# Second mixer of a four-part encoder: exchanging channel rows and step rows by block DMAs instead of TensorE transposes

## The chip, the cores and the metric

The kernel runs on one core of a Trainium2 chip. The metric is the device time of one execution in microseconds (us). Before the change three runs gave a median of 1613.68 us (1609.65 to 1622.86).

Engines are named as the profile names them: PE is TensorE's matmul, PEld its weight load, DVE is VectorE, ACT is ScalarE, POOL is GpSimd. SP issues every DMA of this stage, in one order.

## The reference, cut to what matters

Two layers, each a mixer, cross-attention and a ConvFFN, on 512 steps of 1024 channels. The change lies in the mixer of the second layer:

```python
def mixer_cd(hn, ...):
    u_c, h_d = split_sizes(hn @ w_in, (C_WIDTH, 2 * D_WIDTH))      # 512 and 1024 channels
    u = u_c.reshape(Bn, S, C_NGROUPS, C_GROUP)                     # 32 groups of 16 channels
    y_f = s5_scan(u, ...)                                          # s_t = a s_(t-1) + B u_t ; y_t = Re(C s_t)
    y_b = flip(s5_scan(flip(u), ...))                              # the same backwards
    y = (y_f + y_b).reshape(Bn, S, C_WIDTH) + d_skip * u_c
    z = gelu(y)
    o_c = z * sigmoid(z @ w_glu + b_glu)
    val, gate = split(h_d, 2)                                      # conformer part
    u = depthwise_conv(val * sigmoid(gate), conv_w, conv_b)        # 31 taps
    o_d = silu(layernorm(u, ln_g, ln_b))
    return concatenate([o_c, o_d]) @ w_out
```

All arithmetic is in float32; the large products split each operand into a high and a low part and use three matmuls.

## The kernel before, in words

Activations lie with channels in the 128 partitions and the 512 steps along the free axis. The 512 channels of each part are four blocks of 128 (index i, 0 to 3). In `mixer_cd` a table `CD` (lines 82 to 87) is read from left to right; each entry is a letter (a step) and a digit (the block), and the first instruction that a step puts on PE and on SP is tied behind the last one traced there, so the table sets the order on these two engines. A scheduler orders the rest; the DVE taps (`q`) are tied on DVE.

The letters that matter here, for block i:

- `u`: projection (24 matmuls of 512 columns) of S5's input, scaled on DVE into `uT` (line 1327). `v`, `V` and `g`, `G`: the same for the value and the gate of the conformer part; the gated product ends on DVE at line 1447.
- `a` and `b`: the scan works on pieces of 8 steps. For it a row must be one of 8 steps times 16 channels of a group, and a column one of 64 pieces, eight groups side by side. `a` makes eight transposes on PE (`chunks`, line 1336) with two evictions by ACT (line 1337), `b` eight more (`steps_`, line 1345) with one eviction into `Rg` (line 1353).
- `c`, `C`: 16 matmuls (line 1374) on `Rg`, eviction to `T`, two DMAs that swap the halves of `T` (lines 1378 and 1379), then eight DVE instructions with the scan (lines 1380 to 1388). `s` swaps halves again by DMA (`X2s`, lines 1394 and 1395), `x` adds (line 1402, on POOL for three of the eight).
- `y`: 24 matmuls (lines 1416 and 1418) give S5's output, evicted by ACT. `f` transposes it back, eight transposes (`channels`, line 1425), adds the skip on DVE (line 1431) and applies gelu on ACT (line 1433).
- `q`: two taps of the depthwise convolution of blocks 0 and 1 on DVE, in the channel layout (line 1463). Blocks 2 and 3 go through PE instead: `A` and `B` transpose as `a` and `b` do, `Z` (twice a block) makes 20 matmuls (line 1489) with a table `ct`, `F` transposes back (line 1425) and adds the bias on ACT (line 1497). `N` sums the four blocks for the layernorm's mean (lines 1505 to 1509).
- `l`, `L`, `m`, `w` load tables by DMA (`bm`, `cst`, `cm`, `ct`). `k` is one step of the next cross-attention's keys and values: eight of 12 matmuls of 512 columns (weights `in_w_xv`), then eight of 24 matmuls of 256 columns (`in_w_xk`). These depend on nothing in the mixer.

Weights of 512 KB arrive through three buffers `wr` (line 147). Their DMAs stand in a fixed order among SP's other DMAs. ACT rounds a weight to the high part `wh` (line 201), DVE or POOL makes the low part `wl` (line 202), and PE then uses it (lines 206 to 208). SP issues in order: while a DMA waits for its data, all that stand behind it wait too.

Of the kernel before, what the change touches and what calls it, by code (L numbers as in the profile page):

```python
# [12 lines left out]
F32R = mybir.dt.float32r  # L13
# [6 lines left out]
S = 512  # L20
# [70 lines left out]
def trunk(ctx, tc, xT, memT, pos, vec, amask, cmask, bmask,  # L91
# [9 lines left out]
    n_ = [0]  # L101
# [1156 lines left out]
    def mixer_cd(norm, nnext, kv):  # L1258
# [6 lines left out]
        def k4(shape, tag, bufs, dt=F32):  # L1265
            return T.tile(shape, dt, tag=tag, bufs=bufs, name=nm(tag))
# [3 lines left out]
        g3 = lambda v: v.rearrange("p (g c) -> p g c", c=64)  # L1270
        xp = [T.tile([128, 8, 65], F32, name=f"xp{j}") for j in range(2)]
# [57 lines left out]
        def chunks(src):  # L1329

            us = src.rearrange("p (c t) -> p t c", t=8)
            at = k4([64, 8, 8, 16], "at", 3)
            for hf in range(2):
                tp = tp_ps()
                for t in range(4):
                    PE.transpose(tp[:64, 128 * t:128 * t + 128], us[:, 4 * hf + t], ident)
                A.activation(at[:, :, 4 * hf:4 * hf + 4].rearrange("c g t k -> c t g k"),
                             tp[:64].rearrange("c (t g k) -> c t g k", t=4, k=16), AF.Copy)
            return at

        def steps_(at):

            rp = sc_ps()
            for g in range(8):
                PE.transpose(rp[:, 64 * g:64 * g + 64], at[:, g].rearrange("c t k -> c (t k)"), ident[:64, :64])
            return rp
# [63 lines left out]
        def y_(i):  # L1410
            At[i] = k4([64, 8, 8, 16], "at", 3)
            for hf in range(2):
                yp = sc_ps()
                for g in range(4):
                    o, gg = yp[:64, 128 * g:128 * g + 128], 4 * hf + g
                    PE.matmul(o, Rg[i][:, 64 * gg:64 * gg + 64], cm[i][0][:, gg], start=True, stop=False)
                    for d in range(2):
                        PE.matmul(o, X[i, d][:, gg, d:d + 64], cm[i][1 + d][:, gg], start=False, stop=d == 1)
                A.activation(At[i][:, :, 4 * hf:4 * hf + 4].rearrange("c t g k -> c g t k"),
                             yp[:64].rearrange("c (g t k) -> c g t k", g=4, k=16), AF.Copy)  # L1420

        def channels(at):
            yq = sc_ps()
            for t in range(8):
                PE.transpose(yq[:, 64 * t:64 * t + 64], at[:, t].rearrange("c g k -> c (g k)"), ident[:64, :64])
            return yq
# [110 lines left out]
        stage = {"u": (PS_, u_), "a": (PS_, a_), "b": (PS_, b_), "x": ((), x_), "y": (PS_, y_),  # L1537
# [4 lines left out]
                 "A": (PS_, ca_), "B": (PS_, cb_), "w": (PS_, w_), "Z": (PS_, z_), "q": ((V,), q_), "F": (PS_, cf_), "N": (PS_, n_),  # L1542
# [8 lines left out]
        for i in range(4):  # L1551
            split(hg[i], uT[i])
        for i in range(4):
# [8 lines left out]
            V.scalar_tensor_tensor(sgm, sgm, 1.0, uT[i], op0=ALU.add, op1=ALU.mult)  # L1562
            o_t[i] = k4([128, 2, S], "at" if i < 2 else "bm", 3 if i < 2 else 2, F32R)
# [78 lines left out]
def _col(v):  # L1642
    return np.asarray(v, np.float32).reshape(-1, 128).T


def layout(inp):
# [87 lines left out]
```

## Time and profile before

| | |
|---|---|
| median of three runs | 1613.68 us |
| the profiled execution, its own time | 1613.46 us |
| its span (first to last instruction) | 1611.7 us |
| PE busy | 1562.1 us, 97% |
| PEld busy | 1307.9 us, 81% |
| DVE busy | 1077.3 us, 67% |
| ACT busy | 708.3 us, 44% |
| POOL busy | 358.7 us, 22% |
| granted TensorE clock over the span | 0.984 |
| DMA | 189.11 MB, 117 GB/s on average |

Busy shares are averages over stages with different limits; a matmul's busy time overlaps its neighbours'. What one costs in a stream is the distance from its start to the next one's. `mixer_cd`'s work on PE runs from about 866 us to 1110 us of the span, the part that the change touches from about 874 us to 1062 us.

### The profile page before, as it was taken

The numbers are of one execution on the slowest core, as the hardware profiler recorded it, in microseconds if no ns is written. First come the engines' busy times: TensorE is split into PE (matmuls) and PEld (weight loads), VectorE is DVE, ScalarE is ACT, GpSimd is POOL, SyncE is SP. The second block draws the span as 40 slices with busy tenths as digits, with TensorE's granted clock in tenths as the row PEclk, the third lists the DMA queues.
The fourth block names the chain that finished last, engine by engine and source line by source line (L and its number), as shares of the span: only waits on it lengthen the run. The fifth ranks groups of instructions, "written<-read, shape, count | busy, mean of one in ns | idle before, by whom it ended". The sixth has DMA issues, their size and how long they took to land. (4 is left out here: it accounts for less than half of the span.)

```text
span 1611.7 us, 20961 instructions
## 1 busy us (share of the span) xinstructions
PE 1562.1 (97%) x8036; PEld 1307.9 (81%) x8036; DVE 1077.3 (67%) x1479; ACT 708.3 (44%) x1089; POOL 358.7 (22%) x367
## 2 busy tenths in 40 slices
PE   8999999999999999999999988989999999999997
PEld 6787889888888787777788877978888888888887
DVE  7576766466568789579746997375745766636644
ACT  5464755354444443234336342374534444414423
POOL 8411000000059853553510111110000101100101
PEclk9999999999999999999999998999999999999998
DMA  5322333231223335435454685452302322232331
GB/s 178 109 72 86 118 105 118 66 121 63 66 80 100 111 111 152 144 116 164 126 166 172 218 276 172 150 177 91 106 27 79 105 97 100 92 105 92 89 109 64
DMA packets 76117, 189.11 MB, mean 117 GB/s; under 512 B 8368, under 2 KB 27440, under 8 KB 76016
## 3 DMA queue, kind: packets, MB, share of 16 engines
q1 hardware_dynamic: 75376, 186.58, 36.1%
q8 instruction: 63, 1.03, 0.3%
q0 software_dynamic: 320, 1.05, 0.2%
q14 instruction: 38, 0.31, 0.1%
q10 hardware_dynamic: 320, 0.13, 0.0%
HBM read 162.43 MB, written 19.01 MB: 113 GB/s over the span
## 5 line engine op out<-in xcount | busy, mean ns | idle before, releaser
L201 ACT ACTIVATE wh<-wr 128x1024 fp32r<-128x1024 f32 (+1 forms) x229 | 239.2, 1045 | 430.3 <-PE mm L207 324.2
L208 PE MATMUL mm<-hg,wl 128*128 128x512 f32 x1000 | 394.9, 395 | 12.3 <-DVE wl L202 10.9
L206 PE MATMUL mm<-hg,wh 128*128 128x512 f32 x1000 | 399.2, 399 | 4.6 <-ACT wh L201 4.6
L207 PE MATMUL mm<-hg,wh 128*128 128x512 f32 x1000 | 393.6, 394 | 0.0
L202 DVE TENSOR_TENSOR wl<-wr,wh 128x1024 fp32r<-128x1024 f32 (+1 forms) x219 | 285.7, 1305 | 73.7 <-ACT wh L201 71.6
L208 PEld LDWEIGHTS mm<-hg,wl 128*128 128x128 f32 x1000 | 190.3, 190 | 56.6 <-DVE wl L202 13.7
L206 PEld LDWEIGHTS mm<-hg,wh 128*128 128x128 f32 x1000 | 190.7, 191 | 46.5 <-ACT wh L201 5.0
L207 PEld LDWEIGHTS mm<-hg,wh 128*128 128x128 f32 x1000 | 190.4, 190 | 40.4 <-issue 1.4
L208 PE MATMUL mm<-g,wl 128*128 128x512 f32 x324 | 126.7, 391 | 3.2 <-DVE wl L202 3.1
L206 PE MATMUL mm<-g,wh 128*128 128x512 f32 x324 | 126.9, 392 | 0.0
L207 PE MATMUL mm<-g,wh 128*128 128x512 f32 x324 | 126.2, 389 | 0.0
L976 POOL TENSOR_TENSOR t<-t,t 128x512 f32<-128x512 f32 x22 | 28.9, 1315 | 427.6 <-ACT t L182 427.6
L968 DVE TENSOR_TENSOR u<-mm,R 128x512 f32<-128x512 f32 x88 | 60.3, 688 | 73.8 <-PE mm L208 73.6
L970 ACT ACTIVATE t<-u,vt 128x512 f32<-128x512 f32 x88 | 70.8, 807 | 42.9 <-DVE u L968 42.6
L986 DVE TENSOR_TENSOR h<-mm,h 128x512 f32<-128x512 f32 x40 | 27.6, 691 | 87.7 <-PE mm L208 87.7
L971 DVE SCALAR_TENSOR_TENSOR t<-u,vt,t 128x511 f32<-128x511 f32 x88 | 77.8, 885 | 7.9 <-ACT t L970 7.9
L972 DVE SCALAR_TENSOR_TENSOR t<-u,vt,t 128x511 f32<-128x511 f32 x88 | 76.8, 872 | 4.0 <-DMA dct<-tr 1.4
L208 PEld LDWEIGHTS mm<-g,wl 128*128 128x128 f32 x324 | 60.8, 188 | 16.8 <-DVE wl L202 4.0
L182 ACT ACTIVATE t<-t 128x512 f32<-128x512 f32 x44 | 27.8, 632 | 102.3 <-DVE t L972 102.2
L207 PEld LDWEIGHTS mm<-g,wh 128*128 128x128 f32 x324 | 60.8, 188 | 12.5
L206 PEld LDWEIGHTS mm<-g,wh 128*128 128x128 f32 x324 | 60.9, 188 | 12.4
L202 POOL TENSOR_TENSOR wl<-wr,wh 128x1024 fp32r<-128x1024 f32 x10 | 25.3, 2531 | 148.4 <-ACT wh L201 148.4
(522 smaller groups left out, 3020.2 us busy)
## 6 DMA issues: line engine op xcount, KB each, us to landing
wr<-in_w_up SPq DMA_DIRECT2D x88, 512.0 KB
wr<-in_w_dn SPq DMA_DIRECT2D x32, 448.0 KB
wr<-in_w_ab SPq DMA_DIRECT2D x16, 512.0 KB
wr<-in_w_xv SPq DMA_DIRECT2D x16, 512.0 KB
wr<-in_w_xk SPq DMA_DIRECT2D x16, 512.0 KB
wr<-in_w_xq SPq DMA_DIRECT2D x16, 512.0 KB
wr<-in_w_xo SPq DMA_DIRECT2D x16, 512.0 KB
wr<-in_w_dn SPq DMA_DIRECT2D x16, 512.0 KB
```

Of the source, the lines that this page charges most:

```text
L182: tabbed(A.activation(dst, src, fn, **kw))
L201: A.activation(H[:, :n], raw[:, :n], AF.Copy)
L202: (eng or V).tensor_tensor(L[:, :n], raw[:, :n], H[:, :n].bitcast(F32), ALU.subtract)
L206: PE.matmul(ps, lH, rH, start=start, stop=False)
L207: PE.matmul(ps, lH, rL, start=False, stop=False)
L208: PE.matmul(ps, lL, rH, start=False, stop=stop)
L968: V.tensor_tensor(u, ps, R, ALU.mult)
L970: A.activation(t, u, AF.Identity, scale=vc(f"cw{l}", 44 + i), bias=vc(f"cb{l}", i))
L971: V.scalar_tensor_tensor(t[:, 1:], u[:, :S - 1], vc(f"cw{l}", i), t[:, 1:], op0=ALU.mult, op1=ALU.add)
L972: V.scalar_tensor_tensor(t[:, :S - 1], u[:, 1:], vc(f"cw{l}", 88 + i), t[:, :S - 1], op0=ALU.mult, op1=ALU.add)
L976: (V if l == 0 else G).tensor_tensor(res[1], res[1], res[0], ALU.mult)
L986: V.tensor_tensor(h[c], ps, h[c], ALU.add)
```

## The change

Channels are put into another order within each block (row 8k+g instead of 16g+k for group g, channel k), by reordering the weights and vectors on the host. The steps of `uT` are stored with the place in the piece outermost. A block copy of 16 rows by 8 groups by 64 columns then exchanges rows of channel and rows of step, so `forth` and `back` are eight DMAs each, issued by SP. The transposes and their evictions go. `y` and `Z` take the tables as the stationary operand and the data as the moving one (64 columns instead of 128), and write 128 rows. `e` and `E` are new letters (the way back); `b` and `B` go. DVE and ACT take over the reordering of steps where they read or write. `CD` is written anew.

```diff
 CD = """
-l0 L0 K0 u0 v0 V0 g0 a0 G0 b0 k1 u1 c0 C0 m0 q0 k1 a1 v1 V1 l1 q0 q0 s0 L1 b1 k1 g1 G1 x0 q0 q0 c1 C1 k1 q0 u2 q0 y0
-l2 q0 q1 a2 q1 k1 s1 q0 f0 L2 q1 v2 m1 q0 V2 x1 b2 q1 q0 g2 q0 G2 q1 c2 C2 A2 k1 q0 q1 y1 q0 k1 m2 B2 w2 q1 u3 s2 L3 q0 q1
...
+l0 L0 K0 u0 v0 V0 a0 g0 G0 k1 u1 c0 C0 m0 q0 k1 a1 v1 V1 l1 q0 q0 s0 L1 k1 g1 G1 x0 q0 q0 c1 C1 k1 q0 u2 q0 y0
+l2 q0 q1 k1 a2 q1 s1 q0 L2 q1 v2 m1 q0 V2 x1 e0 q1 q0 g2 q0 G2 q1 f0 c2 C2 k1 A2 q0 q1 y1 q0 k1 m2 w2 q1 u3 s2 L3 q0 q1
...
         def u_(i):
...
-            V.tensor_tensor(uT[i], ps, R, ALU.mult)
...
+            V.tensor_tensor(ct3(uT[i]), tc3(ps), tc3(R), ALU.mult)
+        def forth(dst, src):
+            for t in range(8):
+                nc.sync.dma_start(dst[16 * t:16 * t + 16], src[:, 64 * t:64 * t + 64])
+
+        def back(dst, src):
+            for t in range(8):
+                nc.sync.dma_start(dst[:, 64 * t:64 * t + 64], g3(src[16 * t:16 * t + 16]))
 
         def a_(i):
-            At[i] = chunks(uT[i])
-
-        def b_(i):
             Rg[i] = b2("Rg", 4)
-            A.activation(Rg[i], steps_(At[i]), AF.Copy)
+            forth(g3(Rg[i]), uT[i])
...
         def y_(i):
...
+            yp = sc_ps()
+            for g in range(8):
+                o = yp[:, 64 * g:64 * g + 64]
+                PE.matmul(o, cm[i][0][:, g], Rg[i][:, 64 * g:64 * g + 64], start=True, stop=False)
+                for d in range(2):
+                    PE.matmul(o, cm[i][1 + d][:, g], X[i, d][:, g, d:d + 64], start=False, stop=d == 1)
+            At[i] = b2("sh", 3)
+            A.activation(At[i], yp, AF.Copy)
+
+        def e_(i):
+            y = b2("sd", 2)
+            back(y, At[i])
+            At[i] = y
 
         def f_(i):
-            us = uT[i].rearrange("p (c t) -> p t c", t=8)
-            yq = channels(At[i])
-            V.scalar_tensor_tensor(us, us, vc("s5_d", i), yq.rearrange("p (t c) -> p t c", t=8),
-                                   op0=ALU.mult, op1=ALU.add)
-            A.activation(uT[i], uT[i], AF.Gelu_apprx_tanh)
+            V.scalar_tensor_tensor(uT[i], uT[i], vc("s5_d", i), At[i], op0=ALU.mult, op1=ALU.add)
+            A.activation(Rg[i].rearrange("p (c t) -> p c t", t=8), uT[i].rearrange("p (t c) -> p c t", t=8),
+                         AF.Gelu_apprx_tanh)
...
-            V.scalar_tensor_tensor(dv[i], g, 1.0, dv[i], op0=ALU.add, op1=ALU.mult)
+            if i < 2:
+                V.scalar_tensor_tensor(dv[i], g, 1.0, dv[i], op0=ALU.add, op1=ALU.mult)
+            else:
+                Bt[i] = b2("sh", 3)
+                V.scalar_tensor_tensor(ct3(Bt[i]), tc3(g), 1.0, tc3(dv[i]), op0=ALU.add, op1=ALU.mult)
...
         def ca_(i):
-            Bt[i] = chunks(dv[i])
-
-        def cb_(i):
-            A.activation(vg[i % 2][:, :, 2:66], g3(steps_(Bt[i])), AF.Copy)
+            forth(vg[i % 2][:, :, 2:66], Bt[i])
...
+        def ce_(i):
+            y = b2("sd", 2)
+            back(y, Bt[i])
+            Bt[i] = y
 
         def cf_(i):
-            yq = channels(Bt[i])
             accs[i] = b2("dv", 6)
-            A.activation(accs[i].rearrange("p (c t) -> p t c", t=8), yq.rearrange("p (t c) -> p t c", t=8),
+            A.activation(accs[i].rearrange("p (c t) -> p c t", t=8), Bt[i].rearrange("p (t c) -> p c t", t=8),
                          AF.Identity, bias=vc("conv_b", i))
...
+    q = np.arange(512).reshape(4, 8, 16).transpose(0, 2, 1).reshape(512)
```

SP's order around the weight of `v3` (the first `in_w_cd` below), before the change; `X2s` is the second swap of block 2, `cst` and `bm` are tables of block 3:

```order
L147 DMA wr_8159<-in_w_xv 128x1024
L1394 DMA X2s_8192<-T1s_8015 64x512
L1395 DMA X2s_8192<-T1s_8015 64x512
L1394 DMA X2s_8195<-T1s_8038 64x512
L1395 DMA X2s_8195<-T1s_8038 64x512
L1363 DMA cst_8198<-dct_0_118 128x1024
L1363 DMA cst_8200<-dct_1_119 128x1024
L147 DMA wr_8217<-in_w_cd 128x1024
```

The same place in the changed kernel; `sd` is the way back of `y1`, `Rg` the way forth of `u3`:

```order
L147 DMA wr_8096<-in_w_xv 128x1024
L1339 DMA sd_8199<-sh_8057 128x1x64 x7
L1335 DMA Rg_8165<-uT_8127 16x8x64 x3
L1384 DMA X2s_8129<-T1s_7969 64x512
L1385 DMA X2s_8129<-T1s_7969 64x512
L1335 DMA Rg_8165<-uT_8127 16x8x64
L1384 DMA X2s_8132<-T1s_7992 64x512
L1385 DMA X2s_8132<-T1s_7992 64x512
L1353 DMA cst_8135<-dct_0_118 128x1024
L1353 DMA cst_8137<-dct_1_119 128x1024
L147 DMA wr_8143<-in_w_cd 128x1024
```

Eleven block DMAs, four of which wait for `uT` of block 3, now stand ahead of that weight.

SP's order around the last `in_w_xv` weight, before the change:

```order
L1394 DMA X2s_8518<-T1s_8359 64x512
L1395 DMA X2s_8518<-T1s_8359 64x512
L1394 DMA X2s_8521<-T1s_8382 64x512
L1395 DMA X2s_8521<-T1s_8382 64x512
L147 DMA wr_8548<-in_w_xv 128x1024
```

The same place in the changed kernel; `vg` is the way forth of the gated product of block 3 (`sh`, written at line 1436, which answers to line 1447 before):

```order
L1385 DMA X2s_8423<-T1s_8281 64x512
L1335 DMA vg_7313<-sh_8385 16x8x64 x8
L1384 DMA X2s_8423<-T1s_8281 64x512
L1384 DMA X2s_8426<-T1s_8304 64x512
L1385 DMA X2s_8426<-T1s_8304 64x512
L147 DMA wr_8453<-in_w_xv 128x1024
```

The last weight of this kind, and three of the four swaps of block 3, now stand behind DMAs that wait for the gate's product.

PE's order around the mean's matmul (on `T` and `ones`), before the change; `hg` are matmuls of the GLU:

```order
L206 MATMUL mm_8888<-hg_89,wh_8865 128x512
L207 MATMUL mm_8888<-hg_89,wh_8865 128x512
L208 MATMUL mm_8888<-hg_89,wl_8866 128x512
L1509 MATMUL sc_8834<-T_1456_8830,ones 128x512
L206 MATMUL mm_8913<-hg_86,wh_8909 128x512
```

In the changed kernel; `mg` are matmuls of the last key step ahead of it:

```order
L207 MATMUL mm_8738<-mg_7735,wh_8734 128x256
L208 MATMUL mm_8738<-mg_7735,wl_8735 128x256
L1498 MATMUL sc_8770<-T_1434_8766,ones 128x512
L206 MATMUL mm_8805<-hg_86,wh_8801 128x512
L207 MATMUL mm_8805<-hg_86,wh_8801 128x512
```

Before, 24 matmuls of the GLU stand ahead of the mean's; now none does, and a key step stands in their place.

## Rows read from the trace of the kernel before

**Rows 1.** The page, part 1: busy time, share of the span, instructions.

```profile
PE 1562.1 (97%) x8036; PEld 1307.9 (81%) x8036; DVE 1077.3 (67%) x1479; ACT 708.3 (44%) x1089; POOL 358.7 (22%) x367
```

**Rows 2.** Windows: length, busy PE, PEld, DVE, ACT, POOL, granted clock, DMA share, GB/s.

```profile
890.00:976.00 86.00, 78.94 (x451) 64.70 (x450) 84.36 (x118) 32.81 (x50) 11.20 (x5) 0.96 0.72 245
957.00:976.00 19.00, 12.84 (x53) 9.21 (x52) 18.17 (x24) 6.42 (x9) 4.89 (x2) 0.82 0.65 222
```

**Rows 3.** Waits of PE, 860 to 1110 us: total, times, longest.

```profile
PE mm L206 <- ACT wh L201: 3.5, 1, 3.5
PE tp L1336 <- DVE dv L1447: 2.8, 1, 2.8
```

**Rows 4.** Timeline of PE: start, duration, line, out<-in, shapes, count.

```profile
875.02 1.03 PE L1336 MATMUL tp<-ident,uT 128*64 128x128 f32 x8
875.81 0.48 PE L206 MATMUL mm<-hg,wh 128*128 128x512 f32 x1
...
878.73 0.71 PE L1345 MATMUL sc<-ident,at 64*128 64x64 f32 x8
879.36 0.50 PE L206 MATMUL mm<-hg,wh 128*128 128x512 f32 x1
...
884.94 3.68 PE L1374 MATMUL tp<-Rg,bm 128*128 128x64 f32 x32
...
1025.52 4.53 PE L1489 MATMUL sc<-ct,vg 128*64 128x128 f32 x40
```

**Rows 5.** Timeline of SP: block copies of 64 KB in a row; a pair of swaps.

```profile
828.89 4.37 SPq L1210 DMA_DIRECT2D dmt<-kl  x7
...
986.43 0.59 SPq L1379 DMA_DIRECT2D T1s<-T  x1
```

**Rows 6.** Timeline of DVE: the instruction that waited for that pair.

```profile
989.51 0.69 DVE L1380 TENSOR_TENSOR T<-T,cst 128x512 f32<-128x512 f32 x1 [0.40 <-DMA T1s<-T]
```

**Rows 7.** DVE's lines, 860 to 1110 us: count, busy us, mean ns, idle.

```profile
L1431 DVE SCALAR_TENSOR_TENSOR uT<-uT,vt,sc 128x512 f32<-128x512 f32 x4 | 4.9, 1218 | 0.2 <-PE sc L1425 0.2
L1463 DVE SCALAR_TENSOR_TENSOR dv<-dv,vt,dv 128x497 f32<-128x497 f32 x4 | 2.9, 732 | 0.1
```

**Rows 8.** DMA, 603 to 609 us, eight block copies: packets, MB, share of engines.

```profile
q1 hardware_dynamic: 988, 0.48, 30.6%
```

**Rows 9.** Timelines of DVE, SP and PE ahead of the matmuls of `v3`.

```profile
934.83 1.22 DVE L202 TENSOR_TENSOR wl<-wr,wh 128x1024 fp32r<-128x1024 f32 x1
...
956.16 0.47 SPq L1394 DMA_DIRECT2D X2s<-T1s  x1
...
960.67 0.43 SPq L147 DMA_DIRECT2D wr<-in_w_cd  x1
...
967.19 0.80 PE L206 MATMUL mm<-hg,wh 128*128 128x512 f32 x1 [3.53 <-ACT wh L201]
```

**Rows 10.** Timelines around the gate of block 3: SP, DVE, POOL, PE.

```profile
998.43 0.59 SPq L147 DMA_DIRECT2D wr<-in_w_xv  x1
...
1003.33 1.74 DVE L1447 SCALAR_TENSOR_TENSOR dv<-dg,dv 128x512 f32<-128x512 f32 x1
...
1005.13 1.92 PE L1336 MATMUL tp<-ident,dv 128*64 128x128 f32 x8 [2.79 <-DVE dv L1447]
...
1014.89 2.38 POOL L202 TENSOR_TENSOR wl<-wr,wh 128x1024 fp32r<-128x1024 f32 x1 [10.36 <-ACT wh L201]
```

**Rows 11.** Timelines of PE, ACT and DVE from the last `Z` to the mean.

```profile
1041.35 0.59 ACT L1491 ACTIVATE at<-sc 64x512 f32<-64x512 f32 x1 [3.57 <-PE sc L1489]
...
1044.95 0.50 PE L206 MATMUL mm<-hg,wh 128*128 128x512 f32 x1
1045.06 1.30 ACT L1497 ACTIVATE dv<-sc,vt 128x512 f32<-128x512 f32 x1 [0.90 <-PE sc L1425]
1046.39 0.69 DVE L1507 TENSOR_TENSOR T<-T,dv 128x512 f32<-128x512 f32 x1 [0.64 <-ACT dv L1497]
...
1050.56 1.02 PE L1509 MATMUL sc<-T,ones 128*128 128x512 f32 x2
```

More of the change, by code (lines that the diff above doesn't have):

```diff
@@ L1270, in mixer_cd @@
         g3 = lambda v: v.rearrange("p (g c) -> p g c", c=64)
+        tc3 = lambda v: v.rearrange("p (c t) -> p t c", t=8)
+        ct3 = lambda v: v.rearrange("p (t c) -> p t c", t=8)
         xp = [T.tile([128, 8, 65], F32, name=f"xp{j}") for j in range(2)]
@@ L1326, in u_ @@
             uT[i] = b2("uT", 4)
-            V.tensor_tensor(uT[i], ps, R, ALU.mult)
[L1329 to L1346, printed above, removed]
+            V.tensor_tensor(ct3(uT[i]), tc3(ps), tc3(R), ALU.mult)
[5 more added lines that the diff above has]
+                nc.sync.dma_start(dst[:, 64 * t:64 * t + 64], g3(src[16 * t:16 * t + 16]))
         def a_(i):
-            At[i] = chunks(uT[i])
-        def b_(i):
             Rg[i] = b2("Rg", 4)
-            A.activation(Rg[i], steps_(At[i]), AF.Copy)
+            forth(g3(Rg[i]), uT[i])
         def l_(i):
@@ L1410, in y_ @@
         def y_(i):
[L1411 to L1426, printed above, removed]
-        def f_(i):
-            us = uT[i].rearrange("p (c t) -> p t c", t=8)
-            yq = channels(At[i])
-            V.scalar_tensor_tensor(us, us, vc("s5_d", i), yq.rearrange("p (t c) -> p t c", t=8),
-                                   op0=ALU.mult, op1=ALU.add)
-            A.activation(uT[i], uT[i], AF.Gelu_apprx_tanh)
+            yp = sc_ps()
[10 more added lines that the diff above has]
+            At[i] = y
+        def f_(i):
+            V.scalar_tensor_tensor(uT[i], uT[i], vc("s5_d", i), At[i], op0=ALU.mult, op1=ALU.add)
+            A.activation(Rg[i].rearrange("p (c t) -> p c t", t=8), uT[i].rearrange("p (t c) -> p c t", t=8),
+                         AF.Gelu_apprx_tanh)
         dv = {}
@@ L1484, in z_ @@
             if hf == 0:
-                Bt[i] = k4([64, 8, 8, 16], "at", 3)
+                Bt[i] = b2("sh", 3)
             yp, ts = sc_ps(), [cts.pop(0) for _ in range(2)]
@@ L1488, in z_ @@
                 for j in range(5):
-                    PE.matmul(yp[:64, 128 * g:128 * g + 128], vg[i % 2][:, 4 * hf + g, j:j + 64], ts[g // 2][:, g % 2, j],
+                    PE.matmul(yp[:, 64 * g:64 * g + 64], ts[g // 2][:, g % 2, j], vg[i % 2][:, 4 * hf + g, j:j + 64],
                               start=j == 0, stop=j == 4)
-            A.activation(Bt[i][:, :, 4 * hf:4 * hf + 4].rearrange("c t g k -> c g t k"),
-                         yp[:64].rearrange("c (g t k) -> c g t k", g=4, k=16), AF.Copy)
+            A.activation(Bt[i][:, 256 * hf:256 * hf + 256], yp[:, :256], AF.Copy)
+        def ce_(i):
+            y = b2("sd", 2)
+            back(y, Bt[i])
+            Bt[i] = y
         def cf_(i):
-            yq = channels(Bt[i])
             accs[i] = b2("dv", 6)
-            A.activation(accs[i].rearrange("p (c t) -> p t c", t=8), yq.rearrange("p (t c) -> p t c", t=8),
+            A.activation(accs[i].rearrange("p (c t) -> p c t", t=8), Bt[i].rearrange("p (t c) -> p c t", t=8),
                          AF.Identity, bias=vc("conv_b", i))
@@ L1536, in mixer_cd @@
         PS_ = (PE, nc.sync)
-        stage = {"u": (PS_, u_), "a": (PS_, a_), "b": (PS_, b_), "x": ((), x_), "y": (PS_, y_),
+        stage = {"u": (PS_, u_), "a": (PS_, a_), "e": (PS_, e_), "x": ((), x_), "y": (PS_, y_),
                  "l": (PS_, l_), "L": (PS_, r_), "m": (PS_, m_), "s": (PS_, s_),
@@ L1551, in mixer_cd @@
         for i in range(4):
-            split(hg[i], uT[i])
+            split(hg[i], Rg[i])
         for i in range(4):
@@ L1561, in mixer_cd @@
             tact(sgm, ps, AF.Tanh, scale=0.5, bias=bgh[:, i:i + 1])
-            V.scalar_tensor_tensor(sgm, sgm, 1.0, uT[i], op0=ALU.add, op1=ALU.mult)
-            o_t[i] = k4([128, 2, S], "at" if i < 2 else "bm", 3 if i < 2 else 2, F32R)
+            V.scalar_tensor_tensor(sgm, sgm, 1.0, Rg[i], op0=ALU.add, op1=ALU.mult)
+            o_t[i] = k4([128, 2, S], "ct" if i < 2 else "bm", 2, F32R)
             A.activation(o_t[i][:, 0], sgm, AF.Copy, scale=0.5)
@@ L1689, in layout @@
     a["wg2"] = g2
-    a["w_cd"] = _blocks(f("w_in_cd")[0])
-    a["w_glu"] = _blocks(f("s5_w_glu")[0])
-    a["w_ocd"] = _blocks(f("w_out_cd")[0])
+    a["w_cd"] = _blocks(f("w_in_cd")[0][:, np.concatenate([q, 512 + q, 1024 + q])])
+    a["w_glu"] = _blocks(f("s5_w_glu")[0][q][:, q])
+    a["w_ocd"] = _blocks(f("w_out_cd")[0][np.concatenate([q, 512 + q])])
     lre, lim = (f(n)[0].reshape(64, 64).T for n in ("s5_lam_re", "s5_lam_im"))
```

11 lines of the change are left out of this document (6 added, 5 removed).

## The prediction

> **What bounds the kernel now.** I read the page's busy shares first. PE is busy 97% of the span and the next engine, DVE, 67% [rows 1]; taken alone, this says that PE work taken away is time saved. The window view of the stretch that the change touches says something else: from 890 to 976 us DVE is busy for 84.36 of 86 us, more than PE's 78.94 [rows 2]. There DVE runs convolution taps, the scans, the scaling of projections and the low parts of weights, in an order that is fixed. The waits of PE show the consequence. Its longest wait is for a rounded weight, 3.5 us, and the next for DVE's gated product, 2.8 us [rows 3]. The weight was late because SP, which issues in order, stood before the second swap of block 2 until DVE had finished its operand (956.16), and could issue the weight at 960.67 only; PE took it up at 967.19 [rows 9]. So up to about 967 us the stage goes at the pace of DVE and of SP's order behind it. Behind that DVE has slack, and PE with the weights' arrival sets the pace.
>
> **Removed from PE.** Eight transposes of `a` take 0.79 us from their first start to the next instruction's (875.02 to 875.81), eight of `b` 0.63 us (878.73 to 879.36) [rows 4]; `F` and `f` have the shape of `b`. Six forward ways and six ways back make 6 x 0.79 + 12 x 0.63 = 12.3 us. **Exchanged operands.** The old form of `Z` (64 weight columns, 128 moving) takes 4.53/40 = 0.113 us a record; the new one (128 weight columns, 64 moving) is the form of line 1374, 3.68/32 = 0.115 us [rows 4]. The 352 records of `y` and `Z` therefore gain nothing (0.7 us the other way).
>
> **Evictions and reordering.** ACT loses some 25 evictions and is idle enough not to bound. On DVE the skip becomes contiguous; an access in steps of 8 costs 1218 ns (line 1431), a contiguous one of that kind 732 [rows 7], so `f` gives back 0.5 us, while `uT` and the last two gated products pay 0.5 us each if reading in steps costs what line 1431 shows (nothing, if not). Over the stage DVE is about even.
>
> **Added on SP.** 12 x 8 = 96 DMAs of 32 KB. No such copy stands in the trace; the nearest are the block copies of line 1210 (8 x 16 x 128), seven in 4.37 us, 0.62 us each [rows 5]. A batch of eight is 5.0 us of SP. Landing: a pair of swaps issued by 987.02 was taken by DVE at 989.51, 2.5 us [rows 5, 6]; that DVE instruction had idled, so this is the DMA's. From data to data a way takes 7.5 us. Most of the twelve are covered by other projections on PE; three places are not.
>
> **First half: given back.** Of the 12.3 us, five sets of `a` and seven of `b`'s shape, 8.4 us, lie ahead of the matmuls of `v3` at 967.19. But their weight stays behind the swaps of block 2 in SP's order, and the swaps behind DVE. DVE's chain starts 1.4 us earlier (the first block's `a` and `b` are gone); ahead of the last swap's operand it now has two more taps (2 x 0.66 us, a tap's distance in a run) and the scaling of `u3` (0.7), and SP has one more block copy in between (0.6): together -1.4 + 2.6 = +1.2 us. Low parts move the same way: that of line 202 at 934.83 [rows 9] now has three taps and a gated product more ahead of it, so PE, earlier by its removed transposes, waits for it. I take `v3` at +1 us, with -1.4 (no change of rows matters) and +4 (steps of 8 dear, SP's copies in the way) as ends. So the 8.4 us buy nothing.
>
> **Second half: a new wait for the last values' weight.** Before, PE is done with the work ahead of the transposes of the product at 1005.13 - 2.79 = 1002.34 [rows 10]. Now without a set of transposes (0.6) and with +1, then one `Z` (4.5) and 17 matmuls of 512 columns (24 take 5.6 [rows 11], so 4.0), it reaches the last `in_w_xv` step at 1011.2. That weight was issued at 998.43 [rows 10]; now it stands behind eight copies of the gated product of block 3 and three swaps. The product was made from 1003.33 on [rows 10]: +1, 1.2 for steps of 8, 5.0 for the copies, 1.7 for three swaps, 0.4 for its own issue: 1012.6. With 2.5 to land, 1.05 to round and 2.38 for POOL's low part [rows 10]: 1018.5. The wait is 7.3 us. The wait for the product itself, 2.8 us, is gone; it is already in the 1002.34. **TensorE's clock.** After the wait of 3.53 us the granted clock was 0.82 over 19 us, the lower level (1.2 GHz) for 0.36 of them and 3.4 us of full clock lost, part of it while PE idled [rows 2, 9]; I take 2 us for the new wait, from 0 to 3.4.
>
> **The end: the last way back.** From 1018.5: this step 2.8, clock 2, `y` 48 x 0.115 = 5.5, `Z` 4.5, two key steps 5.6 (24 matmuls of 256 columns at half of 5.6), `Z` 4.5, so 1043.4. Then eviction 0.6, eight copies 5.0, landing 2.5, bias 1.3, sum 0.7 [rows 5, 6, 11]: the mean's matmul at 1053.5. The two key steps behind `Z` cover 5.6 of these 10.1 us; 4.5 are a wait. Before, the mean stood at 1050.56 with 5.6 us of GLU done ahead of it [rows 11]; that GLU now comes behind. So the stage is 1053.5 + 5.6 - 1050.56 = 8.5 us late. What follows (the GLU, keys, output projection) is the same work in the same order.
>
> **Sum.** The profiled execution took 1613.46 us, 0.2 below the median of the runs; plus 8.5 makes **1622 us**. The ends of this case: with `v3` at -1.4, landings 0.6 shorter and no clock loss, 1616; with `v3` at +4, 3.4 for the clock and once more 2 at the end, 1629.
>
> **A rule against the change.** The pieces of these copies are 256 bytes long. The eight copies of line 1210, in pieces of 512 bytes, used 30.6% of 16 engines over 6 us for 988 packets, 30 ns a packet [rows 8]; 1024 pieces of a batch at that price are 1.9 us of all engines, well within its 5.0 us of issue. The Trainium skill, "DMA: Bandwidth & Descriptors", section "Specifications", wants 512 bytes for line rate and says that below it the engine reads, modifies and writes. No row here prices that. By the page, with the packet's price doubled as my estimate, a batch would be 3.8 us, still under the issue; the sum would stay, and rival 2 below would be likelier.
>
> **The rivals.**
> 1. *PE sets the pace throughout* (0.17). Then 12.3 us, the wait of 2.8 and the clock's 3.4 go, 18.5 in all, less up to 13 (the 4.5 at the end and the new weight's wait): between 1595 and 1608, 1601 in the middle. For it: 97% busy. Against it: the 84.36 of 86 us of DVE, and the two weights that stay behind DVE's results.
> 2. *The copies crowd out the weights* (0.20), slower than before. Place: SP from 948 to 961 us and the DMA engines, 72% busy from 890 to 976 us [rows 2]. Six batches fall there: at 1.9 us they bring the engines to 85%, so weights still pass, and at double that price, the bound that I set for pieces half as long, to 99%. If `u3` is scaled only at 958, four of its copies and both swaps come behind it, and the weight of `v3` is issued after 963. It decides from there on: `v3` 5 us late instead of 1, the last weight behind busy engines another 3 to 5, and a second low clock, 2 to 3: 1632 to 1645, 1636 in the middle.
> 3. *The transposes don't leave the path* (0.03): if the exchanged `y` and `Z` cost more than their shape says, 352 records at, say, 0.03 more, 10 us: 1630 and more. The order on PE shows the transposes gone, and rows 4 price the form; I keep little for it.
>
> **Chances and range.** The forecast's case, given back and a little more, 0.60. A measurement tells about 1% from no change: 1597.5 to 1629.8. Below lies some of rival 1, 0.07; above rival 2 nearly whole, rival 3 and 0.04 of the first case, 0.25; the rest, 0.68, is within. For eight in ten I reach from 1603 (0.08 of rival 1 left out) to 1637 (half of rivals 2 and 3, 0.11); the likeliest case alone is 1616 to 1629.
>
> **What would show it.** In the profile after: PE still near its old end of the first half, with a new wait of some 8 us for DVE's low part near 930 us and a longer one before `v3`, at 966 to 971 us; DVE busy almost all of 890 to 976; SP waiting before the copies of block 3's product, and PE waiting some 7 us for the rounded or low part of the last `in_w_xv`; some 4 us before the mean's matmul, ended by DVE. Block copies issued every 0.6 us and landing within 3. I am wrong in the first half if `v3` starts before 962, and in the second if the last values' step isn't waited for. If copies land later than 5 us after issue, rival 2 is at work.

## The result, and the profile after

| | before | after |
|---|---|---|
| median of ten runs each on one chip | 1620.4 us (1609.37 to 1623.37) | 1629.99 us (1626.61 to 1641.02) |
| ratio after to before, 95% interval | | 1.0106 [1.0084, 1.0127] |
| profiled execution: span | 1611.7 us | 1639.2 us |
| stage: line 251 to the output projection's first matmul | 210.2 us | 229.2 us |
| at 1.2 GHz within the stage | 10.2 us | 54.6 us |

The change makes the kernel about 1.06% slower, some 17 us. The two medians alone give 1.0059, because the ten runs of the kernel before fall here into two groups, four of 1609 to 1614 us and six of 1619 to 1623 us; beside the experiments its median was 1613 to 1616 us. The profiled execution after is the slowest of its ten, the one before is among the faster of its kernel, and 11.6 of the 27.5 us between their spans stand ahead of the stage (line 251 starts at 866.0 and at 877.6), most of them in stretches of low clock (47.8 us at 1.2 GHz there, 27.3 before). So "the stage" below is counted from the last matmul of line 251; times "behind line 251" count from there (the expectations of the first runs count from the matmul before, 0.4 us earlier). It grew by 19.0 us.

The page's first part, after, against [rows 1]:

```profile
PE 1570.5 (96%) x7892; PEld 1316.2 (80%) x7892; DVE 1076.3 (66%) x1479; ACT 697.8 (43%) x1067; POOL 360.5 (22%) x367
```

PE issues 144 matmuls fewer and is busy for longer: at the lower clock the same matmul takes longer. The windows of the stage show it (length, busy PE, PEld, DVE, ACT, POOL, granted clock, DMA share, GB/s); the first line is after, the second the kernel before:

```profile
877.00:1107.00 230.00, 196.71 (x1097) 168.38 (x1096) 155.72 (x212) 83.45 (x116) 30.79 (x13) 0.88 0.60 190
```

```profile
866.00:1076.00 210.00, 195.79 (x1238) 167.37 (x1236) 157.94 (x214) 93.72 (x138) 29.90 (x13) 0.98 0.56 192
```

PE is busy for nearly as long in both (196.71 and 195.79 us): what the transposes took, the lower clock takes. Its idle time rose from 14.2 to 33.3 us, which is the whole growth of the stage. PE's waits in the stage after (total, times, longest), against [rows 3]:

```profile
PE mm L206 <- ACT wh L201: 16.4, 5, 5.6
PE sc L1498 <- DVE T L1496: 5.4, 1, 5.4
PE mm L207 <- POOL wl L202: 3.0, 2, 1.8
PE tp L1364 <- ACT dg L1431: 2.9, 1, 2.9
```

Rounded weights were waited for once before, 3.5 us; now five times, 16.4 us. The longest of these waits, and the others of note, in PE's timeline after:

```profile
914.20 0.66 PE L1364 MATMUL tp<-Rg,bm 128*128 128x64 f32 x2 [2.87 <-ACT dg L1431]
976.43 0.80 PE L206 MATMUL mm<-wh,mg 128*128 128x512 f32 x1 [5.33 <-ACT wh L201]
987.94 0.79 PE L206 MATMUL mm<-hg,wh 128*128 128x512 f32 x1 [3.86 <-ACT wh L201]
1035.41 0.80 PE L206 MATMUL mm<-wh,mg 128*128 128x512 f32 x1 [5.60 <-ACT wh L201]
1048.25 4.63 PE L1475 MATMUL sc<-vg,ct 128*128 128x64 f32 x40
1076.94 1.19 PE L1498 MATMUL sc<-T,ones 128*128 128x512 f32 x1 [5.43 <-DVE T L1496]
```

The matmuls of `v3` start at 987.94, 110.4 us behind line 251, where before it was 101.2 [rows 9]. What holds the weights stands in SP's timeline, in order of time:

```profile
886.96 5.81 SPq L1335 DMA_DIRECT2D Rg<-uT  x8
892.88 1.00 SPq L147 DMA_DIRECT2D wr<-in_w_cd  x2
...
964.46 0.90 SPq L1462 DMA_DIRECT2D ct<-in_ctab  x2
965.46 0.38 SPq L147 DMA_DIRECT2D wr<-in_w_xv  x1
965.93 8.20 SPq L1339 DMA_DIRECT2D sd<-sh  x7
975.30 1.90 SPq L1335 DMA_DIRECT2D Rg<-uT  x3
977.31 0.53 SPq L1384 DMA_DIRECT2D X2s<-T1s  x1
...
981.57 0.43 SPq L147 DMA_DIRECT2D wr<-in_w_cd  x1
...
1022.88 5.11 SPq L1335 DMA_DIRECT2D vg<-sh  x8
...
1029.95 0.59 SPq L147 DMA_DIRECT2D wr<-in_w_xv  x1
...
1068.12 5.05 SPq L1339 DMA_DIRECT2D sd<-sh  x8
```

Each weight (`wr`) here is issued behind a batch of copies, the one at 965.46 behind a batch and five tables. Seven copies of `e1` take 5.05 us elsewhere for eight, but 8.20 here: three were issued as an earlier DMA landed, a table of 512 or 640 KB. The wait view of SP for 964 to 984 us names them:

```profile
SPq L1339 <- DMA ct<-in_ctab: 2.4, 2, 1.4
SPq L1339 <- DMA cm<-dc: 1.1, 1, 1.1
SPq L1335 <- DMA wr<-in_w_xv: 1.1, 1, 1.1
```

In each of these cases it was the DMA issued eight places earlier, as in all 17 places of this trace where a DMA of SP was released by the landing of another: the compiled order of waits lets a DMA of SP go only when the eighth before it has landed.

### The profile page after: what moved, and what is told of

Read it like the earlier page. It is cut to its first block, busy times and chain, and to the rows that moved or that the text cites. A ratio compares the mean times of both kernels' runs of the same rounds, so it can differ in the third digit from the quotient of the medians.

```text
span 1639.2 us, 20785 instructions
## 1 busy us (share of the span) xinstructions
PE 1570.5 (96%) x7892; PEld 1316.2 (80%) x7892; DVE 1076.3 (66%) x1479; ACT 697.8 (43%) x1067; POOL 360.5 (22%) x367
## 4 chain that ended last, share of the span: by engine, by line
PE 64%; DVE 14%; POOL 6%; DMA 5%; ACT 4%; SPq 4%; issue 3%; ACTq 0%; DVEq 0%; POOLq 0%
PE mm L208 18%; PE mm L206 18%; PE mm L207 18%; DVE wl L202 3%; PE mm L737 2%; DVE t L971 1%; DMA wr<-in_w_cd 1%; DVE t L972 1%; SPq L1339 1%; ACT wh L201 1%; PE tp L724 1%; DMA T1s<-T 1%; DVE u L968 1%; DVE t L976 1%; POOL t L1139 1%
## 5 line engine op out<-in xcount | busy, mean ns | idle before, releaser
L208 PE MATMUL mm<-hg,wl 128*128 128x512 f32 x1000 | 395.9, 396 | 14.2 <-DVE wl L202 12.8
```

The costliest lines, as they stand in the source:

```text
L208: PE.matmul(ps, lL, rH, start=False, stop=stop)
```

## The experiments

All were timed in five rounds beside the kernel before. The stage and its time at 1.2 GHz are of the one profiled execution. (The "15.4 us at half speed" in e9's expectation is the clock lost, half of e1's 30.7.) The theories are named by letters where an expectation first puts them: Q, D and V in e1, P and W in e5, R in e9, S in e13.

| run | ratio to before, 95% interval | stage, us | at 1.2 GHz, us |
|---|---|---|---|
| e1 no copies | 0.9988 [0.9969, 1.0008] | 214.0 | 30.7 |
| e2 copies from ACT | 1.0027 [1.001, 1.0044] | 214.4 | 34.1 |
| e3 gate's weight first | 1.0101 [1.0072, 1.013] | 226.7 | 51.2 |
| e4 a sixteenth of the bytes | 1.0065 [1.0042, 1.0089] | 225.4 | 54.6 |
| e5 before, half the taps | 0.9985 [0.9967, 1.0004] | 206.2 | 3.4 |
| e6 no copies, half the taps | 0.998 [0.9962, 0.9998] | 207.2 | 17.1 |
| e7 way through DRAM | 1.0111 [1.0083, 1.0138] | 231.6 | 51.2 |
| e8 key step before copies | 1.0039 [1.0018, 1.0059] | 218.6 | 37.5 |
| e9 no copies, weights first | 0.9912 [0.9878, 0.9946] | 196.9 | 13.7 |
| e10 ACT copies, weights first | 0.9966 [0.9945, 0.9988] | 203.8 | 27.3 |
| e11 before, weights first | 0.9967 [0.9943, 0.999] | 207.0 | 6.8 |
| e12 SP copies, two places turned | 1.0057 [1.0031, 1.0083] | 220.5 | 41.0 |
| e13 all eight tied | 1.0112 [1.009, 1.0133] | 225.0 | 44.4 |
| e14 tied, weights first | 1.0087 [1.0066, 1.0107] | 225.6 | 47.8 |
| e15 back from ACT | 1.0027 [1.0009, 1.0045] | 216.0 | 37.5 |
| e16 forth from ACT | 1.0016 [0.9994, 1.0039] | 210.0 | 17.1 |
| e17 copies from POOL | 1.0009 [0.999, 1.0028] | 208.2 | 27.3 |
| e18 DRAM, three queues | 1.012 [1.0087, 1.0152] | 224.9 | 47.8 |

### What the copies cost, and what of them

```
e1   forth/back:  8 x nc.sync.dma_start  ->  A.activation(dst, g3(src) or src, AF.Copy)
e2   nc.sync.dma_start(...)              ->  nc.scalar.dma_start(...)
e3   CD: u0 v0 V0 a0 g0 G0               ->  u0 v0 V0 g0 a0 G0
e4   src[:, ...] to dst[16t:16t+16]      ->  src[8t:8t+8, ...] to dst[16t:16t+1]   (back alike)
```

**e1.** 

> Left out: the exchange itself. One ACT copy per way stands in place of the eight DMAs, so the data is in the wrong rows; all other work is that of the changed kernel. Theory Q (SP's one order: the copies' issue time and their waits for data hold the weights behind them, PE waits and its clock falls): the stage from the norm's matmul (line 251) to the output projection falls from 229 us to below the 210.6 of the kernel before, 200 to 207; ratio to the kernel before 0.993 to 0.998. Rival D (the DMA engines are crowded by 256-byte pieces): the same here. Rival V (the loss is in what the change put on the engines: DVE and ACT reading and writing in steps of 8, the exchanged matmuls): the stage stays at 222 or more; ratio 1.006 or more. If DVE alone sets the pace of the first half, v3 starts no earlier than in the kernel before (101.7 us behind line 251) and only the second half gains.

**e2.** 

> The same 96 copies, issued by ACT in place of SP; all of the work is done. Theory Q: the weights no longer stand behind copies that wait; the stage falls from 229 us to 212 to 218, ratio 0.999 to 1.004 (ACT gains some 60 us of issue in 250, where it was 44% busy, so part may come back as late high parts of weights). Rival D: same bytes, same pieces, so the stage stays at 226 to 232, ratio 1.009 to 1.013. Rival V: the same as D.

**e3.** 

> One step of the table moves: the first block's copies (a0) behind the first gate's projection (g0), so that the next two weights are issued ahead of the copies. Theory Q: the early part goes back: no 2.9 us wait ahead of the matmuls of line 1364 near 914 us and no low clock behind it (some 3 to 4 us), v3 starts 3 to 7 us earlier than 110.3 behind line 251; ratio 1.006 to 1.009. Rivals D and V: within 0.002 of the changed kernel's 1.0106.

**e4.** 

> The same 96 DMAs in the same places on SP, but each takes one row of 16 by 8 pieces instead of 128 pieces, so 1/16 of bytes and pieces; the other rows of the destinations keep a constant set once, so that data is left out. Theory Q: if an issue takes SP its 0.60 us whatever its size, the stage stays at 223 to 230 us, ratio 1.007 to 1.011. Rival D: the engines are free, the stage falls to 200 to 212, ratio at most 1.001. If the issue is cheaper with fewer pieces (the trace shows it), Q expects a gain in proportion: at 0.3 us an issue about half of the way to the run without copies.

Without the exchange the loss is gone (1.0106 to 0.9988, some 19 us), so V falls. But 12.3 us fewer on PE give nothing that can be measured against the kernel before; Q's 0.993 to 0.998, with a stage of 200 to 207 us, was missed too. From ACT's queue, with the same bytes and pieces, two thirds of what the copies cost go: that part was SP's queue. The last third, 1.0027 to 0.9988, is not parted: e1 and e2 differ in the bytes, in the time that a way takes to land and in ACT's work. With a sixteenth of the bytes only 0.4% goes. There an issue takes as long as with all of them (SP's timeline of e4; 0.68 us a copy):

```profile
944.81 0.70 SPq L1344 DMA_DIRECT2D vg<-sh  x1
947.39 4.76 SPq L1344 DMA_DIRECT2D vg<-sh  x7
```

So D explains at most the smaller part. e3 changed nothing that can be measured, but its edit did half of what was meant: one of the two weights went ahead of the copies, the other was issued 15.3 us behind line 251 (15.9 after). What the 2.9 us at 914 wait for, the profile puts down to ACT's `dg`, which that matmul does not read. The semaphore updates in the trace name the table `bm`: issued at 907.91, behind the second batch and a weight, it had landed at 913.90, and the matmul started at 914.20; the last block copy that it needs had landed at 911.38. In e3 that table was issued only 0.4 us earlier, and the wait stayed.

### Why no copies are no gain: DVE, or the weights

```
e5, e6   for k in taps[k0:done[i]]:  ->  for k in taps[k0:done[i]:2]:     (e6 on top of e1)
e8       CD: G3 k1 m3 A3 q1 s3 q1 Z2 k1 w3   ->  G3 k1 m3 k1 s3 q1 A3 q1 Z2 w3
e9       on e1:   y1 q0 k1 m2 w2 q1 u3 s2 L3 q0 q1 k1 l3  ->  y1 q0 k1 u3 m2 w2 q1 q0 q1 k1 s2 L3 l3,  and e8
e10      e2 with e9's table;   e11  before, with the first line of e9
e12      after, with  k1 u3 m2 w2 q1 s2 L3,  and e8
```

**e5.** 

> Left out: every second tap of the DVE convolution, 30 of 60 (some 20 us of DVE at 0.66 us each), in the kernel before. Theory P (in the first half DVE's order sets the pace, which is why the run without copies gained nothing): the second swap of block 2 is issued earlier than 92.3 us behind line 251 and the 3.5 us wait ahead of v3 goes; the stage falls from 210 us to 202 to 207; ratio 0.995 to 0.998. Rival W (DVE is not the bound, the weights come no earlier for another reason): within 0.002 of 1.

**e6.** 

> Left out: the same 30 taps, and the exchange (one ACT copy per way in place of eight DMAs), in the changed kernel. Theory P: with DVE out of the way the 12.3 us of removed transposes come out; the stage is 8 to 12 us shorter than with half the taps in the kernel before, ratio lower than that run's by 0.005 to 0.008. Rival W: no better than the run of the kernel before with half the taps, within 0.002.

**e8.** 

> The table in the second half: the key and value step behind G3, and the swaps of block 3, come ahead of the forward copies of block 3's gated product (m3 k1 s3 q1 A3 q1 Z2 w3 in place of m3 A3 q1 s3 q1 Z2 k1 w3). Theory Q: the last in_w_xv weight is issued before the copies, some 10 us earlier, the waits for it (5.6 and 1.2 us) and the low clock behind them go; the stage falls by 5 to 9 us, ratio 1.004 to 1.008. Rival D or V: within 0.002 of 1.0106. If the wait only moves to the next weight or to the mean at the end, it shows there and the gain is under 3 us.

Theory P falls as the reason why no copies are no gain. In e5 the 3.5 us wait ahead of `v3` goes and the stage is 4.0 us shorter, as P asked, but the time shows no gain that can be told from none. And with 20 us less on DVE the two kernels still differ by 0.0005, each known to 0.0018, where P asked for 0.005 to 0.008. PE's waits stay in e6, where the weights behind the tables are waited for (11.9 us in all, the longest 6.4). e8 holds: the key step and the swaps of block 3, put ahead of a batch in the second half, give back 10.6 us of the stage (1.0106 to 1.0039), and the 5.6 us wait is gone. So about half of the loss lay there. Together they lead to theory R. In e1, SP issues a weight at 949.68 behind five tables, and PE waits for it at 962.08, 12.4 us later; the weight of `v3` (967.55) stands behind swaps that wait for DVE, and PE waits at 975.04. First SP's rows of e1, then PE's:

```profile
947.20 0.33 SPq L1396 DMA_DIRECT2D cm<-dmt  x1
947.63 0.85 SPq L1396 DMA_DIRECT2D cm<-dc  x2
948.54 1.05 SPq L1460 DMA_DIRECT2D ct<-in_ctab  x2
949.68 0.61 SPq L147 DMA_DIRECT2D wr<-in_w_xv  x1
961.09 0.47 SPq L1382 DMA_DIRECT2D X2s<-T1s  x1
...
967.55 0.38 SPq L147 DMA_DIRECT2D wr<-in_w_cd  x1
```

```profile
962.08 1.22 PE L206 MATMUL mm<-wh,mg 128*128 128x512 f32 x2 [5.31 <-ACT wh L201]
964.67 0.79 PE L207 MATMUL mm<-wl,mg 128*128 128x512 f32 x1 [1.37 <-POOL wl L202]
975.04 0.80 PE L206 MATMUL mm<-hg,wh 128*128 128x512 f32 x1 [5.99 <-ACT wh L201]
```

**e9.** 

> Left out: the exchange (as in the run without copies, one ACT copy per way). Three places of the table are turned so that a weight is issued ahead of what held it: the in_w_xv weight behind k1 ahead of block 2's tables cm and ct (2.8 MB), the weight of v3 ahead of the swaps of block 2, and the second half's key step as in the earlier run. Theory R (the transposes' time was given back to weights that stand in SP's order behind tables and swaps, where PE now arrives earlier): the waits of 5.7 us at 94.6, 6.4 at 107.6 and 4.3 at 153.3 us behind line 251 go with the low clock behind them (15.4 us at half speed); the stage falls from 214 us to 199 to 206, ratio 0.990 to 0.995. Rival (DVE's chain or the bandwidth sets the pace): the waits only move; ratio 0.997 or more.

**e10.** 

> All of the work is done: copies issued by ACT, and the same three places of the table turned. Theory R: the stage falls from 214 us to 202 to 210, ratio 0.993 to 0.999, a version that beats both kernels if it is under 0.998. Rival (ACT's queue, where copies wait for data and high parts of weights stand behind them): 1.000 to 1.004 as without the turned places.

**e11.** 

> Control: the first two of the three turned places in the kernel before (transposes on PE; the third has no counterpart there). Theory R: there PE arrives later and waits 3.5 us for v3's weight and little for the other, so the gain is at most 2 to 5 us, ratio 0.997 to 0.999. If the turned places alone are worth as much as in the kernel without copies (0.990 to 0.995), they have nothing to do with the transposes.

**e12.** 

> All of the work is done, copies on SP: the changed kernel with the in_w_xv weight ahead of block 2's tables, and the second half's key step turned (the swaps of block 2 stay where they are). Theory Q and R together: against the run with the second half alone (1.0039) the wait of 6.4 us at 97 us behind line 251 goes, and perhaps some of the one behind it: ratio 0.999 to 1.002. Rival (the wait moves to v3's weight, which still stands behind e1's copies and the swaps): 1.003 to 1.005.

R holds. With the weights ahead, e9 is 0.9912, and its stage 17.1 us shorter than e1's. The waits in e9's stage:

```profile
PE mm L207 <- DVE wl L202: 3.9, 2, 2.7
PE mm L208 <- POOL wl L202: 2.3, 2, 1.5
PE mm L206 <- ACT wh L201: 2.3, 3, 1.2
```

The rounded weights fell from 16.5 us (e1) to 2.3. The first two of the three places turned in the kernel before (e11; the third has no counterpart there) give 0.9967, so of e9's gain over a third is the order alone; 10.1 us of stage separate the two, most of the 12.3 us of transposes. e10 beats both kernels, but only as e11 does: with copies from ACT the change is worth nothing over the transposes. e12 went as its rival said, a little beyond its 1.003 to 1.005: one wait for a weight is 14.2 us long there, and the gain of e8 is not improved.

### What on the queue costs: place, number or latency

```
e13  nc.sync.dma_start(...) -> pinned((nc.sync,), nc.sync.dma_start, ...)     e14: with e9's table
e15  e14, but back by nc.scalar (not tied)        e16  e14, but forth by nc.scalar (not tied)
e17  after by nc.gpsimd, with e9's table
e7   nc.sync.dma_start(d, src);  nc.sync.dma_start(dst, d.rearrange("(k g) (t c) -> t k g c", ...))
e18  e7 with e9's table, out by nc.sync (forth) or nc.scalar (back), in by nc.gpsimd
```

**e13.** 

> All of the work is done, copies on SP. In the changed kernel only the first copy of a step is tied to its place in the table; seven of e1's eight copies and three of a3's went ahead of the swaps of block 2 and of v3's weight, and stood there from 88 to 99 us behind line 251, partly for the landing of the 2.8 MB of tables issued just before. Here each copy is tied behind the one before it, so e1's and a3's come behind v3's weight. Theory S (the step 'v3 at +1' failed because of these ten copies): the swaps of block 2 go from 99.7 to 93 to 96, v3's weight from 104.0 to 96 to 100, the stage falls by 3 to 8 us; ratio 1.005 to 1.009. Rival (the tables' landing or DVE hold them anyway): v3's weight stays at 102 or later, ratio within 0.002 of 1.0106.

**e14.** 

> All of the work is done, copies on SP, each tied to its place, and the three turned places of the table. Theories R and S: the stage falls from 229 us to 206 to 214; ratio 0.997 to 1.003. Rival (SP's 58 us of issue are too much wherever they stand): 1.004 or more, as with two turned places and free copies (1.0057).

**e15.** 

> All of the work is done: the copies back are issued by ACT, which has just made their source by its own eviction; the copies forth stay on SP, each tied; the three turned places. Theory Q: SP keeps half of its copies, ACT waits for little; the stage falls to 200 to 206, ratio 0.993 to 0.998, as good as all copies from ACT (0.9966) or better. Rival (the forward copies on SP, which wait for DVE, are the costly half): 0.999 to 1.004.

**e16.** 

> The mirror image: copies forth issued by ACT, copies back on SP, each tied; the three turned places; all of the work is done. Theory Q: SP no longer waits for DVE's products ahead of weights, but ACT does, ahead of its high parts; ratio 0.996 to 1.001. If the forward copies on SP are the costly half, this run is better than its mirror image by 0.003 or more.

**e17.** 

> All of the work is done: all 96 copies issued by POOL, with the three turned places of the table. Theory Q (a batch costs whatever stands behind it on the issuing queue): POOL is 22% busy, what stands behind is some low parts and three of the eight adds; if an issue there is 0.5 to 0.7 us as POOL's own DMAs of line 793 show, the stage falls to 200 to 208, ratio 0.993 to 0.999, like copies from ACT (0.9966). Rival (an issue of 128 pieces costs POOL's own work, 1 us or more, or slows DVE): 1.000 or more.

**e7.** 

> All of the work is done; each way is two DMAs on SP (256 KB out to DRAM, 256 KB back in the new order) in place of eight, 24 in place of 96. Theory Q with the issue as the price (0.60 us each, whatever the size): SP spends 14 us less 0 to 36 for twelve landings of 2.5 to 3 us that the second DMA waits for, in place of 58; the stage falls from 229 us to 214 to 224, ratio 1.001 to 1.007. Rival D (engines): twice the bytes and the same pieces, so no better than the changed kernel, 1.010 to 1.015.

**e18.** 

> All of the work is done: a way is two DMAs through DRAM, out from SP (forth) or ACT (back), back in the new order from POOL, so that neither SP nor ACT waits for a landing; three turned places of the table. Theory Q: 24 issues over three queues leave SP with six; the stage falls to 198 to 206, ratio 0.992 to 0.998, near the run without copies (0.9912). Rival (the second trip's latency, 5 us and more a way, is on the path from u to the matmuls of c): 0.999 or more.

S falls, as its rival said: tied, `e1`'s copies do stand behind `v3`'s weight, but that weight goes 102.7 us behind line 251 (104.0 after), and the loss stays. SP's timeline of e13:

```profile
958.88 0.43 SPq L147 DMA_DIRECT2D wr<-in_w_xv  x1
965.56 0.51 SPq L1384 DMA_DIRECT2D X2s<-T1s  x1
...
969.20 0.38 SPq L147 DMA_DIRECT2D wr<-in_w_cd  x1
...
970.74 7.24 SPq L189 DMA_DIRECT2D Rg<-uT  x8
```

SP now stands idle from 959.3 to 965.5 for DVE's operand, which is itself late: the matmuls of block 2 (line 1364) start 76.8 us behind line 251, not 69.5 as after or 66.5 as before. PE had waited 4.7 and 3.4 us ahead of them, where after it waits 2.9. The edit ties all twelve batches, so it moves more than `e1`'s and `a3`'s copies; which of them delays what is not traced. e14 agrees that the place is not all: with all eight tied and the weights first it is still 1.0087, as its rival said.

With e9's table the price by queue is then: all on SP 1.0087, half of them off SP 1.0027 (back on ACT) and 1.0016 (forth on ACT), all on POOL 1.0009, all on ACT 0.9966, none 0.9912. e15 and e16 overlap, so neither half is shown the dearer. Q asked for more each time: e15, e17 and e18 fell in their rivals' ranges, e16 just above Q's, and e7 in D's. Why POOL is dearer than ACT, with a shorter issue (0.53 us), stays open. e7 and e18 show that fewer issues do not help when the way gets longer: in e7 SP waited 32.1 us for the trips out of the ways back to land, and in e18, where nothing on SP waits for that, PE waited 8.6 us for one forward way. SP's waits of e7, and PE's of e18:

```profile
SPq L1346 <- DMA dx<-sh: 32.1, 6, 8.2
```

```profile
PE tp L1371 <- DMA Rg<-dx: 8.6, 1, 8.6
```


## Why the prediction went wrong

The time, 1629.99 us, lies within the range of 1603 to 1637, which was wide enough for a loss and for none. The forecast was 8.5 us slower, too little to be told from no change; the kernel is some 17 us slower, clear of noise, to which 0.25 was given. Of the stage's 19.0 us, 9.1 lie ahead of `v3` and 9.9 behind it, where 1 and 7.5 were forecast, so the miss is mostly in the first half. Step by step:

- **Removed from PE, exchanged operands, DVE's steps of 8: right.** `Z` takes 4.63/40 = 0.116 us a record (0.115 forecast). `uT` in steps of 8 takes 1.09 us (0.68 before), and the skip 0.75 in its two undisturbed cases, as assumed. That the transposes are worth their time on PE, e9 against e11 suggests; e9 also has a third place turned.
- **Added on SP: the issue right, its place wrong.** 0.64 us a copy, a batch 5.05 to 5.81 us. But "most of the twelve are covered by other projections on PE" looked at the data alone. What stands behind a batch on SP pays for it too, and a batch behind tables takes 8 us, not 5, since it waits for their landing. The Trainium skill, "DMA: Bandwidth & Descriptors", "Issuing engines are not separate DMA queues", says that issuing from several engines saves only the time of the issue, usually small beside the DMA. Whether it saves no more is not shown: e2 took both the issue and the waits for data off SP. That it is small does not hold here: a copy's 144 packets (128 of them pieces) at the 21 ns below are 0.19 us of 16 engines, its issue is 0.60.
- **"I take `v3` at +1 us": the step that failed.** It came at +9.1 (110.4 against 101.2), beyond the upper end of +4. The sum was -1.4 (DVE's chain for block 2 starts earlier), +2.0 (more work within it) and +0.6 (one more copy on SP). At the last swap, where it was to hold, the same parts measure +4.5, +1.6 and +3.3. Rows of the kernel before, then after; SP's rows are the last of the first swaps of block 2 and the last pair of its second swaps, DVE's the first and the last step of the chain between them:

```profile
940.42 0.59 SPq L1379 DMA_DIRECT2D T1s<-T  x1
942.88 0.69 DVE L1380 TENSOR_TENSOR T<-T,cst 128x512 f32<-128x512 f32 x1
957.52 0.68 DVE L1388 TENSOR_TENSOR T1s<-T1s,cst 128x512 f32<-128x512 f32 x1
958.23 0.46 SPq L1394 DMA_DIRECT2D X2s<-T1s  x1
```

```profile
956.28 0.59 SPq L1369 DMA_DIRECT2D T1s<-T  x1
958.96 0.69 DVE L1370 TENSOR_TENSOR T<-T,cst 128x512 f32<-128x512 f32 x1 [0.86 <-DMA T1s<-T]
975.20 0.69 DVE L1378 TENSOR_TENSOR T1s<-T1s,cst 128x512 f32<-128x512 f32 x1
979.23 0.54 SPq L1384 DMA_DIRECT2D X2s<-T1s  x1
```

  The chain starts at 81.4 us behind line 251, not 76.9: the matmuls of block 2 come 3.0 us later, and SP issues the first swaps between copies of two batches, the last at 78.7, not 74.5. The operand is done at 98.3, not 92.2. Then the swap waits 3.3 us more, since ten copies stand ahead of the second swaps and one between them, as the order ahead of the prediction shows; one was counted. The copies on SP are not all of it: `v3` comes at 107.6 without any (e1), where PE, earlier by its transposes, waits 5.31 and 5.99 us for weights behind tables and swaps, and at 111.8 with the copies on ACT (e2). That the first half gives everything back was right, and the reason in part wrong: less work on DVE sends `v3`'s weight earlier but hardly changes the time (e5 and e6 against before and e1); weights issued ahead of tables and swaps do (e9). The wait of 8 us near 930 for DVE's low part did not appear.
- **A new wait for the last values' weight: right.** Forecast 7.3 us; 5.60 and 1.20 (POOL's low part) measured. e8 removes it, moving the swaps too, and gains 10.6 us of stage, so with the clock it was worth more than its length.
- **TensorE's clock: mis-sized.** 2 us were taken, 3.4 at most. The time at 1.2 GHz rose from 10.2 to 54.6 us, which is up to 22 us of full clock, part of it while PE idled. The waits at 914, at 976 and 988, at 1035 and at 1077 each have such a stretch, of 10 to 20 us; I counted one of them.
- **The end: right.** 5.4 us ahead of the mean (4.5 forecast).
- **Rival 2** named the right place and sign, with its condition met (`v3`'s weight was issued 104.0 us behind line 251; the rival asked for 97). The sign set for it came as well: by the semaphore updates in the trace 25 of the 96 copies landed more than 5 us after their issue (median 2.65). But engines crowded by small pieces are at most the smaller part (e4). Each of the 25 was issued with two to six larger DMAs (256 to 640 KB) under way; with a sixteenth of the bytes 21 of 96 are still as late (e4); and the weights `in_w_cd` landed no later than before (median 5.2 us after issue, 6.7 before). In e2 the copies had a queue of their own (q10), which shows their packets alone, with their share of 16 engines over 214 us:

```profile
q10 hardware_dynamic: 13824, 3.15, 8.5%
```

  That is 291 us of one engine, 21 ns a packet, where pieces of 512 bytes, on their way to DRAM, took 30 [rows 8]. The Trainium skill, "DMA: Bandwidth & Descriptors", "Specifications", would have small pieces read, modified and written; the doubled price that I estimated from it is not seen here. A later section of that page, "Why small descriptors are slow (HBM only)", exempts transfers within SBUF, which these are, and the trace agrees with that one. A batch costs the engines 1.5 us, and a sixteenth of the bytes changed little (e4).
- **Rival 1** needed more than the change: without copies, and with the table written for PE's earlier arrival, the time is near its 1601 us (e9, 1600.15). Its "up to 13" is 11.8 by its own two terms. **Rival 3** fell with V: a record of `Z` costs what its shape says.

## What to carry to other kernels

Work moved from a busy engine to a DMA queue that issues in order was paid for here by whatever stood behind it there: list, for each batch, the next weight on that queue, and what the batch itself must wait for. Time taken off the busiest engine appeared only when the loads were issued earlier as well; before giving the removed work a price, look where the engine will now arrive ahead of its next load. Count each new wait with a stretch of low clock behind it.

## What was not expected of the hardware

- A block copy cost its queue about the same at both sizes tried: 0.60 us of SP for 32 KB, 0.64 for 2 KB (e4). From POOL the median was 0.53 us, from ACT 0.61.
- Packets of 256-byte copies within SBUF took 21 ns (e2), less than those of 512-byte copies to DRAM (30 ns, [rows 8]).
- Taking 20 us of work off DVE, busy for 98% of a stretch of 86 us [rows 2], moved the time by 0.15%, within what can be told from nothing (e5).
